# The last four row chunks of an FFN output: from plain products to a seven-product group of eight

## The chip, the cores and the metric

The kernel runs on one core of a Trainium2 chip. The core has five engines that work side by side and meet at semaphores: TensorE (PE, matmuls; PEld is its loading of weights), VectorE (DVE), ScalarE (ACT), GpSimd (POOL) and SyncE (SP). Transfers are issued from the queues of SP, ACT and POOL. The metric is device time in microseconds, the median of several runs.

## The reference

One layer of a streaming encoder over 1024 tokens with 1024 channels, all in f32: a modulation from `c`, a mixing sub-layer of two causal convolution branches, and a feed-forward (FFN) sub-layer, each added to `x`; at the end an RMS norm. The part that matters here:

```python
x = x + g1 * mix
h2 = rms_norm(x, norm_ffn_g[l]) * (1.0 + sc2) + sh2
a, bgate = jnp.split(jnp.einsum('bsd,df->bsf', h2, w_ffn_in[l]), 2, axis=-1)
x = x + g2 * jnp.einsum('bsf,fd->bsd', jax.nn.silu(a) * bgate, w_ffn_out[l])
...
return rms_norm(x, final_norm_g)
```

The hidden width is 2816, which is 22 row chunks of 128. The output of the FFN is a product of (22 chunks x 1024 tokens) with (22 chunks x 1024 output channels).

## The kernel before, in words

**Operands.** Channels lie on the 128 partitions and tokens along the row; the 1024 tokens are two halves of 512. Each f32 operand is split into a high and a low part that TensorE takes as fp32r, so one block of a product is three matmuls: high by high, low by high, high by low (`mm3`, lines 394, 395 and 397). Weights are loaded into raw buffers by SP, cast to the high part by ACT (line 231), and the low part is formed by DVE (line 232).

**Seven products.** Most matrix products go by a scheme of Strassen's kind: a 2 x 2 block product from seven block products instead of eight. A "dual" is such a block product for two sets of output rows; its products are named 1 to 7 and run in the order `PRODUCTS = "1265734"`. Operand and weight sums are made beforehand (for weights by `dual_units`: three sums before product 6, one before product 3). Products 1, 6, 7, 4 add up in the banks "x", 5 and 3 in the banks "z", 2 goes to "y"; after each product DVE reads the bank and adds it, scaled, into the residual. As 7 adds into the banks that 6 left, and 3 into those of 5, PE can't begin a product before the earlier one of its banks has been read.

**The in stage.** Eleven duals (`in_product`, d = 0 to 10) make the 22 hidden chunks, a pair of them each. After each dual, `hid_set(d)` stores the pair to DRAM scratch: for d up to 8 it forms four sums and makes seven stores, the seven operands that the out stage's products want. The last two pairs (`2 * d >= REST`) are stored plainly, four stores each. A store is a cast (ACT, line 434), a subtraction (DVE, line 435) into one of three "stage" buffers, and a DMA from POOL's queue (line 1314). While the last dual runs, `group_load(0, m)` begins to load operands for the out stage, also from POOL's queue (line 1340).

**The residual.** Right after the in stage, POOL's queue loads x after the mixing sub-layer, eight tiles `x1` (two at line 1398, earlier; six at line 1403 in the order 4, 5, 2, 3, 6, 7). Those six lie in a pool that is opened when the pools "gi" (work tiles of the in stage) and "stage" are closed; the pools are opened so that each tile waits for the very tiles that it lies on.

**The out stage.** Three groups (`GROUPS`) of `GROUP = 3` pairs, that is 18 row chunks; per group two duals (d = 0 for outputs 0, 1, 4, 5; d = 1 for 2, 3, 6, 7) with 7 products of 18 matmuls of 512 tokens (line 397 and its fellows). DVE's `out_evac` (line 1410) adds each bank to x1. The operands of a group (`to`) lie in the pool "t" of 58 tiles of 512 columns; those of the next group are loaded as buffers come free.

**The pieces.** The last four chunks (`REST` to `FC`) are multiplied plainly, from weights `ws` split ahead of time, in three pieces of tokens, `PIECES`: 512, 256 and 256. For each piece and each of eight outputs `piece_out` runs 4 x 3 matmuls, adds the result to x1 (line 1461), squares it (ACT, line 1464) and sums the squares (DVE, line 1473). The final norm and the scaled output of one piece run beside the matmuls of the next (`piece_norm`, `piece_rstd`, `piece_scale`); those of the last piece come after the last matmul, with POOL scaling outputs `POOL_LAST` and DVE the others.

**What sets the order.** The program gives each engine's instructions in the order of the program text where they are ready, and passes over those that are not; `tc.issue_after` forces an order in places. Weights come from a list `plan`; `next_w` keeps two units prepared ahead of the product that runs. In the end every engine and every DMA queue runs its own list in order, so whatever waits at the head of a queue holds all behind it.

Of the kernel before, what the change touches and what calls it, by code (L numbers as in the profile page):

```python
# [120 lines left out]
PIECES = [(0, 512), (512, 256), (768, 256)]  # L123


FILL = 248
# [1 line left out]

@with_exitstack
def block_kernel(ctx: ExitStack, tc: tile.TileContext, x0, xT, c, vecs, ada, w_first, w_plain, w_duals,  # L130
                 w_short, w_conf, w_o, w_fi, w_fo, w_last, outT):
    nc = tc.nc

    def pool(name, bufs, **kw):
# [14 lines left out]
    rawp = pool("raw", 3)  # L149
# [51 lines left out]
    def modc(i):  # L201
        return mod[:, i : i + 1]
# [1 line left out]

    raws = [rawp] * 3 + [rawbp] * 2

    def raw_tile(n=1024):

        raws.append(raws.pop(0))
        return raws[-1].tile([P, 1024], F32, tag="raw", name="raw")[:, :n]  # L210

    def load(src, n=1024):
        raw = raw_tile(n)
# [126 lines left out]
    plan = [None] * KC  # L340
# [14 lines left out]
    def next_w(ahead=AHEAD):  # L355

        fetch(ahead + 1)
        return ready.pop(0)
# [27 lines left out]
    def mm3(outs, wsl, w, xs, first, last, again=False):  # L386

        if w[1] is None:
            for ps, x in zip(outs, xs):
                mm3.ins = nc.tensor.matmul(ps, w[0][:, wsl], x, start=first, stop=last, skip_group_check=again).ins  # L390
            return
        wh, wl = w[0][:, wsl], w[1][:, wsl]
        for ps, (xh, xl) in zip(outs, xs):
            nc.tensor.matmul(ps, wh, xh, start=first, stop=False, skip_group_check=again)  # L394
            nc.tensor.matmul(ps, wh, xl, start=False, stop=False, skip_group_check=again)  # L395
        for ps, (xh, _) in zip(outs, xs):
            mm3.ins = nc.tensor.matmul(ps, wl, xh, start=False, stop=last, skip_group_check=again).ins  # L397
# [32 lines left out]
    def t_pair(name):  # L430
        return hl_tile(name + "h"), hl_tile(name + "l")

    def t_split(src, hi, lo):
        t_split.act = nc.scalar.copy(hi, src).ins  # L434
        t_split.ins = nc.vector.tensor_tensor(lo, src, f32(hi), ALU.subtract).ins  # L435
# [873 lines left out]
    def store(key, src):  # L1309

        s = stagep.tile([P, T], F32R, tag="stage", name="stage")
        t_split(src, s[:, :H], s[:, H:])
        hid_dram[key] = dram.tile([P, T], F32R, name="hid" + "_".join(map(str, key)))
        nc.gpsimd.dma_start(hid_dram[key], s)  # L1314

    def hid_set(d):

        (b11, b12), (b21, b22) = ((ha[2 * d + p, "4"], ha[2 * d + p, "6"]) for p in range(2))
        if 2 * d >= REST:
            for p, half in enumerate(((b11, b12), (b21, b22))):  # L1320
                for h in range(2):
                    store((2 * d + p, h), half[h])
            return
        store((d, "1"), b11)
        store((d, "2"), b21)
        t2 = gip.tile([P, H], F32, tag="g", name="t2")
        nc.vector.tensor_tensor(b11, b11, b12, ALU.subtract)
        minus(t2, b11, b22)
        store((d, "6"), t2)
        store((d, "5"), b11)  # L1330
        nc.vector.tensor_tensor(b12, b22, b12, ALU.subtract)
        store((d, "7"), b12)
        store((d, "3"), b22)
        minus(b21, t2, b21)
        store((d, "4"), b21)

    def t_load(key):
        hl = t_pair("t")
        for t, s in zip(hl, halves):
            nc.gpsimd.dma_start(t, hid_dram[key][:, s])  # L1340
        return hl
# [1 line left out]
    to = {}  # L1343

    def group_load(g, m):
        to[g, m] = [t_load((g * GROUP + i, m)) for i in range(GROUP)]

    def in_product(d, m, between=None):
        late = EARLY[d] == 1
# [20 lines left out]
    for i, (d, m) in enumerate(in_order[5:]):  # L1370
        if i < 4:
            norm_2_sums("5734"[i])
        elif i == 4:
            close(*phase_1)
            raws.append(open_pool("raw_a", 1, side="right", stack=ctx)[1])
            x1aps = [s2p, open_pool("x1a", 1, side="right", stack=ctx)[1]]
            phase_2 = [open_pool("gi", 7), open_pool("stage", 3, side="right")]
            gip, stagep = (p for _, p in phase_2)
        with ExitStack() as order:
            if d < 2:  # L1380
                order.enter_context(tc.issue_after(mm3.ins))
            in_product(d, m)
        if m == PRODUCTS[-1]:
            if 2 <= d < 6:
                with tc.issue_after(in_evac.ins):
                    for b in range(40 + 2 * (d - 2), 42 + 2 * (d - 2)):
                        modulation(b, x1aps[b % 2].tile([P, T], F32, tag="x1", name="ada"))
            if d:
                hid_set(d)
        elif (d, m) == (1, "6"):  # L1390
            hid_set(0)
# [20 lines left out]
            )  # L1412
        return evac

    hid = {}
    n = 2 * GROUP * P
    for g in range(GROUPS):
        for d in range(2):
            units = dual_units([w_fo[g, d, m] for m in range(4)], n)
            plan += [units[m] for m in PRODUCTS]  # L1420
    for g in range(GROUPS):
        for d in range(2):
            banks = {}
            for m in PRODUCTS:
                product(banks, m, to[g, m], out_evac(d))
                if d == 0 and m == "1":
                    if g < GROUPS - 1:
                        for q in PRODUCTS:
                            group_load(g + 1, q)
                    else:  # L1430
                        for h in range(2):
                            for f in range(REST, FC):
                                hid[f, h] = t_load((f, h))


    ws = {}
    for f in range(REST, FC, 2):
        for oh in range(2):
            raw = load(w_last[(f - REST) // 2, oh])
            for d in range(2):  # L1440
                ws[f + d, oh] = t_pair("lw")
                t_split(raw[:, d * H : (d + 1) * H], *ws[f + d, oh])

    LAST = len(PIECES) - 1

# [3 lines left out]
    def on_pool(i, j):  # L1449
        return i < LAST or j in POOL_LAST  # L1450

    def piece_out(i, j):
        at, n = PIECES[i]
        h, off = at // H, at % H
        o = ps_tile("y")[:, :n]
        for f in range(REST, FC):
            xs = tuple(t[:, off : off + n] for t in hid[f, h])
            c0 = (j % 4) * P
            mm3([o], slice(c0, c0 + P), ws[f, j // 4], [xs], f == REST, f == FC - 1)
        dst = x1[j][:, at : at + n]  # L1460
        evac = nc.vector.scalar_tensor_tensor(out=dst, in0=o, scalar=modc(40 + j), in1=dst, op0=ALU.mult, op1=ALU.add)
        piece_out.ins = evac.ins
        sq = wide_tile("sq")[:, :n]
        act = nc.scalar.activation(sq, dst, AF.Square, scale=1.0 / 32.0)
        if i == LAST and j == KC - 1:
# [3 lines left out]
        sqs.append(sq)  # L1469

    def piece_sum(i, j):
        with tc.issue_after(piece_out.ins):
            nc.vector.tensor_tensor(sqs[0], sqs[0], sqs[j], ALU.add)

    def piece_scale(i, rf):
# [39 lines left out]
    for i in range(len(PIECES)):  # L1515
        acc, sqs = sqs[0] if i else None, []
        lag = LAG if i == LAST else 0
        for j in range(KC):
            piece_out(i, j)
            if j > lag and j - lag < KC - APART * (i == LAST):  # L1520
                piece_sum(i, j - lag)
            if i and j == NORM_AT:
                norm = piece_norm(i - 1, [acc])
            if i and j == NORM_AT + 2:
                with tc.issue_after(piece_out.ins):
                    rf = piece_rstd(i - 1, *norm)
                piece_scale(i - 1, rf)
    piece_scale(LAST, piece_rstd(LAST, *piece_norm(LAST, [sqs[0]] + sqs[KC - APART :])))


# [69 lines left out]
```

## Time and profile before

| | us |
|---|---|
| median of 3 runs (lowest, highest) | 1468.06 (1467.23, 1470.21) |
| the profiled execution: its time | 1467.47 |
| the profiled execution: its span | 1465.7 |
| PE busy | 1452.6 |
| DVE busy | 1181.2 |
| ACT busy | 624.5 |
| POOL busy | 505.7 |

The span runs from the first to the last instruction; the profiled execution's time is 1.8 us longer. The profile is a page with busy times, the chain of work that ended last, and groups of instructions by line; behind it one can ask for the instructions of an engine in order of time (start, duration, engine, line, operation, and in brackets the idle time before it and what ended that), for one tile or line, and for busy times by stretch. In a row of stretches the columns are the stretch, its length, and the busy time of PE, PEld, DVE, ACT and POOL, each with its count, then the granted clock, the busy share of the DMA engines and GB/s. Matmuls overlap, so their spacing, not their duration, is the price of one.

### The profile page before, as it was taken

The numbers are of one execution on the slowest core, as the hardware profiler recorded it, in microseconds if no ns is written. First come the engines' busy times: TensorE is split into PE (matmuls) and PEld (weight loads), VectorE is DVE, ScalarE is ACT, GpSimd is POOL, SyncE is SP. The second block draws the span as 40 slices with busy tenths as digits, with TensorE's granted clock in tenths as the row PEclk, the third lists the DMA queues.
The fourth block names the chain that finished last, engine by engine and source line by source line (L and its number), as shares of the span: only waits on it lengthen the run. The fifth ranks groups of instructions, "written<-read, shape, count | busy, mean of one in ns | idle before, by whom it ended". The sixth has DMA issues, their size and how long they took to land.

```text
span 1465.7 us, 17762 instructions
## 1 busy us (share of the span) xinstructions
PE 1452.6 (99%) x6418; PEld 1192.7 (81%) x6418; DVE 1181.2 (81%) x1642; ACT 624.5 (43%) x911; POOL 505.7 (35%) x460
## 2 busy tenths in 40 slices
PE   9999999999999999999999999999999999999997
PEld 5788888888888888888888888888888888888887
DVE  8897999987988979999787798777777665676755
ACT  4873333333333346455225474434444343222335
POOL 0007777677767761111012002101111015435005
PEclk9999999999999999999999999999999999999999
DMA  9442222323222367485585337655554449989403
GB/s 369 172 156 82 73 101 72 115 72 101 72 101 58 130 204 269 130 267 191 198 326 191 118 116 238 221 181 193 169 170 149 146 155 373 353 276 288 137 11 115
DMA packets 85498, 251.38 MB, mean 172 GB/s; under 512 B 9841, under 2 KB 12529, under 8 KB 85410
## 3 DMA queue, kind: packets, MB, share of 16 engines
q1 hardware_dynamic: 44368, 142.04, 29.2%
q0 software_dynamic: 37008, 95.63, 19.7%
q10 hardware_dynamic: 4034, 12.59, 2.3%
q8 instruction: 50, 0.82, 0.2%
q14 instruction: 38, 0.31, 0.1%
HBM read 187.82 MB, written 62.39 MB: 171 GB/s over the span
## 4 chain that ended last, share of the span: by engine, by line
PE 88%; DVE 1%; POOL 1%; issue 1%; DMA 0%; ACT 0%; POOLq 0%; DVEq 0%
PE bank L397 11%; PE bank L394 11%; PE bank L395 11%; PE x L395 8%; PE x L397 8%; PE x L394 8%; PE z L395 4%; PE z L394 4%; PE z L397 4%; PE y L394 3%; PE y L395 3%; PE y L397 3%; PE mix L394 2%; PE mix L395 2%; PE yb L395 2%; PE yb L397 2%
## 5 line engine op out<-in xcount | busy, mean ns | idle before, releaser
L231 ACT CAST wh<-raw 128x1024 fp32r<-128x1024 f32 (+3 forms) x256 | 256.4, 1003 | 469.7 <-PE bank L395 145.9
L232 DVE TENSOR_TENSOR wl<-raw,wh 128x1024 fp32r<-128x1024 f32 (+3 forms) x176 | 201.1, 1143 | 54.0 <-ACT wh L231 52.7
L232 POOL TENSOR_TENSOR wl<-raw,wh 128x1024 fp32r<-128x1024 f32 x80 | 194.0, 2427 | 103.9 <-ACT wh L231 100.7
L964 DVE SCALAR_TENSOR_TENSOR c<-diff,vec,c 128x512 f32<-128x512 f32 x232 | 168.3, 751 | 2.7
L1314 POOL DMA_DIRECT2D hid<-stage x71 | 37.8, 533 | 344.7 <-DVE stage L435 340.7
L397 PE MATMUL bank<-th,wl 128*128 128x512 f32 x312 | 121.6, 390 | 0.3 <-POOL wl L232 0.3
L395 PE MATMUL bank<-tl,wh 128*128 128x512 f32 x312 | 121.5, 390 | 0.0
L394 PE MATMUL bank<-th,wh 128*128 128x512 f32 x312 | 121.5, 389 | 0.0
L964 DVE SCALAR_TENSOR_TENSOR c<-u,wsum,c 128x512 f32<-128x512 f32 x112 | 84.3, 753 | 2.3
L397 PEld LDWEIGHTS bank<-th,wl 128*128 128x128 f32 x312 | 58.6, 188 | 12.8 <-POOL wl L232 0.7
L395 PEld LDWEIGHTS bank<-tl,wh 128*128 128x128 f32 x312 | 58.6, 188 | 12.2
L394 PEld LDWEIGHTS bank<-th,wh 128*128 128x128 f32 x312 | 58.6, 188 | 12.0
L434 ACT CAST stage<-g 128x512 fp32r<-128x512 f32 x62 | 38.3, 621 | 63.5 <-DMA hid<-stage 40.2
L435 DVE TENSOR_TENSOR stage<-g,stage 128x512 fp32r<-128x512 f32 x62 | 42.4, 689 | 26.9 <-ACT stage L434 26.8
L309 POOL TENSOR_TENSOR raw<-raw 128x1024 f32<-128x1024 f32 x8 | 20.5, 2561 | 109.7 <-ACT th L434 104.7
L397 PE MATMUL x<-th,wl 128*128 128x512 f32 x144 | 56.1, 390 | 0.0
L395 PE MATMUL x<-tl,wh 128*128 128x512 f32 x144 | 56.1, 389 | 0.0
L394 PE MATMUL x<-th,wh 128*128 128x512 f32 x144 | 56.1, 389 | 0.0
L1340 POOL DMA_DIRECT2D th<-hid x71 | 38.1, 536 | 51.4 <-PE x L397 33.1
L397 PE MATMUL yb<-zsh,wl 128*128 128x512 f32 x128 | 49.9, 390 | 0.0
L394 PE MATMUL yb<-zsh,wh 128*128 128x512 f32 x128 | 49.9, 389 | 0.0
L395 PE MATMUL yb<-zsl,wh 128*128 128x512 f32 x128 | 49.8, 389 | 0.0
(817 smaller groups left out, 4175.1 us busy)
## 6 DMA issues: line engine op xcount, KB each, us to landing
hid<-stage POOLq DMA_DIRECT2D x71, 512.0 KB, 4.8
raw<-in_w_duals SPq DMA_DIRECT2D x57, 512.0 KB, 3.5
raw<-in_w_fi SPq DMA_DIRECT2D x54, 512.0 KB, 4.5
th<-hid POOLq DMA_DIRECT2D x71, 256.0 KB, 5.6
tl<-hid POOLq DMA_DIRECT2D x71, 256.0 KB, 5.7
ada<-in_ada SPq DMA_DIRECT2D x24, 512.0 KB, 5.7
raw<-in_ada SPq DMA_DIRECT2D x24, 512.0 KB, 4.8
raw<-in_w_fo SPq DMA_DIRECT2D x24, 384.0 KB, 5.8
```

The source lines that it names most:

```text
L231: hi = nc.scalar.copy(wh, raw)
L232: lo = lo_engine.tensor_tensor(wl, raw, f32(wh), ALU.subtract)
L309: unit.eng.tensor_tensor(out, x, y, ALU.add)
L394: nc.tensor.matmul(ps, wh, xh, start=first, stop=False, skip_group_check=again)
L395: nc.tensor.matmul(ps, wh, xl, start=False, stop=False, skip_group_check=again)
L397: mm3.ins = nc.tensor.matmul(ps, wl, xh, start=False, stop=last, skip_group_check=again).ins
L434: t_split.act = nc.scalar.copy(hi, src).ins
L435: t_split.ins = nc.vector.tensor_tensor(lo, src, f32(hi), ALU.subtract).ins
L964: tap.ins = nc.vector.scalar_tensor_tensor(out=out, in0=src[:, s : s + H], scalar=wt, in1=acc, op0=ALU.mult, op1=ALU.add).ins
L1314: nc.gpsimd.dma_start(hid_dram[key], s)
L1340: nc.gpsimd.dma_start(t, hid_dram[key][:, s])
```

## The change

All 22 chunks of the FFN's output go by seven products, in groups of 3, 4 and 4 pairs (`GROUPS = 3, 4, 4`). The plain rest with its weights `w_last` is gone, and so are the plain stores: all eleven pairs make four sums and seven stores each.

The first two groups run as before, the second with 24 matmuls per product and weights of 1024 columns. The last group runs in another order: products 1, 2, 6, 7, 4 of dual 0, then the same of dual 1 (512 tokens each), and then products 5 and 3 of both duals in the two pieces of 256 tokens: 5 of dual 0, 5 of dual 1, 3 of dual 0, 3 of dual 1. After 2 and 4 the outputs of the first half of the tokens are complete, after 5 and 3 those of a piece, in the order 4, 5, 6, 7, 0, 1, 2, 3; `piece_done` then does what `piece_out` did behind its matmuls. `POOL_LAST` becomes 1, 4, 7.

The weights of products 5 of dual 1 and 3 of both duals stay in the three weight buffers over both pieces. Those of 5 of dual 0 are split into four tiles of the pool "t" instead (`split_5`), ahead of the sums for product 6 of dual 1, whose first sum takes the raw buffer that held them.

```diff
-POOL_LAST = (0, 3, 5)
+POOL_LAST = (1, 4, 7)
-GROUP, GROUPS = 3, 3
-REST = 2 * GROUP * GROUPS
+GROUPS = 3, 4, 4
+FIRST = [sum(GROUPS[:g]) for g in range(len(GROUPS))]
+LAST_PRODUCTS = "12674"
...
     def hid_set(d):
-        if 2 * d >= REST:
-            for p, half in enumerate(((b11, b12), (b21, b22))):
-                for h in range(2):
-                    store((2 * d + p, h), half[h])
-            return
         store((d, "1"), b11)
...
+    def last_units(mats, first):
+        a, homes = {}, dict(zip(("11", "12", "21", "22"), (rawp, rawbp, rawp, rawp) if first else (rawap, rawp, rawp, rawp)))
...
+            if m == "6":
+                if not first:
+                    split_5()
+                a["s1"] = raw_tile(home=rawbp)
+                add(a["s1"], a["21"], a["22"])
+                add(a["21"], a["21"], a["11"])
+                add(a["11"], a["11"], a["s1"])
+            w = split_w(a[{"1": "11", "2": "12", "6": "11", "7": "21", "4": "22", "5": "s1", "3": "12"}[m]], 1024)
+            if m == "6":
+                add(a["12"], a["12"], a["11"])
+            return w
...
+    def split_5():
+        for p in range(2):
+            w5.append(t_pair("w5"))
+            t_split(last[0]["a"]["s1"][:, p * H : (p + 1) * H], *w5[p])
...
+    plan += [last[d][m] for d in range(2) for m in LAST_PRODUCTS]
+    plan += [last[d][m] for m, d in (("5", 1), ("3", 0), ("3", 1))]
...
+    def piece_product(banks, d, m, i):
+        at, n = PIECES[i]
+        off = at % H
+        apart = (d, m) == (0, "5")
+        for p in range(2):
+            if m == "5":
+                banks[d, p] = ps_tile("z")[:, :n]
+            ps = banks[d, p]
+            for k in range(KH):
+                xs = tuple(t[:, off : off + n] for t in to[FINAL, m][k])
+                c0 = ((0 if apart else p) * KH + k) * P
+                mm3([ps], slice(c0, c0 + P), w5[p] if apart else ws[d, m], [xs], m == "5" and k == 0, k == KH - 1, m == "3")
+            last_evac(d, i)(p, m, ps)
...
+    for d in range(2):
+        banks = {}
+        for m in LAST_PRODUCTS:
+            product(banks, m, to[FINAL, m], last_evac(d, 0))
+    ws = {}
+    for i in range(1, len(PIECES)):
+        banks = {}
+        for m in "53":
+            for d in range(2):
+                if i == 1 and (d, m) != (0, "5"):
+                    ws[d, m] = next_w()
+                piece_product(banks, d, m, i)
```

More of the change, by code (lines that the diff above doesn't have):

```diff
@@ L205, in block_kernel, with raw_tile, load @@
     raws = [rawp] * 3 + [rawbp] * 2
[L207 to L213, printed above, removed]
+    def raw_tile(n=1024, home=None):
+        if home is None:
+            raws.append(raws.pop(0))
+        return (home or raws[-1]).tile([P, 1024], F32, tag="raw", name="raw")[:, :n]
+    def load(src, n=1024, home=None):
+        raw = raw_tile(n, home)
         with tc.issue_after(x1_load[0]) if x1_load else ExitStack():
@@ L1345, in group_load @@
     def group_load(g, m):
-        to[g, m] = [t_load((g * GROUP + i, m)) for i in range(GROUP)]
+        to[g, m] = [t_load((FIRST[g] + i, m)) for i in range(GROUPS[g])]
     def in_product(d, m, between=None):
@@ L1413, in out_evac, with add, unit @@
         return evac
-    hid = {}
-    n = 2 * GROUP * P
-    for g in range(GROUPS):
+    def last_units(mats, first):
+        a, homes = {}, dict(zip(("11", "12", "21", "22"), (rawp, rawbp, rawp, rawp) if first else (rawap, rawp, rawp, rawp)))
+        def add(out, x, y):
+            nc.vector.tensor_tensor(out, x, y, ALU.add)
+        def unit(m):
+            if m == "1":
+                for i, (b, home) in enumerate(homes.items()):
+                    a[b] = load(mats[i], home=home)
+            if m == "6":
[9 more added lines that the diff above has]
+            return w
+        return {m: (lambda m=m: unit(m)) for m in PRODUCTS} | {"a": a}
+    def split_5():
+        for p in range(2):
+            w5.append(t_pair("w5"))
+            t_split(last[0]["a"]["s1"][:, p * H : (p + 1) * H], *w5[p])
+    w5 = []
+    FINAL = len(GROUPS) - 1
+    for g in range(FINAL):
+        n = 2 * GROUPS[g] * P
         for d in range(2):
-            units = dual_units([w_fo[g, d, m] for m in range(4)], n)
+            units = dual_units([(w_fo0[d, m] if g == 0 else w_fo1[g - 1, d, m]) for m in range(4)], n)
             plan += [units[m] for m in PRODUCTS]
-    for g in range(GROUPS):
+    last = [last_units([w_fo1[FINAL - 1, d, m] for m in range(4)], d == 0) for d in range(2)]
+    plan += [last[d][m] for d in range(2) for m in LAST_PRODUCTS]
+    plan += [last[d][m] for m, d in (("5", 1), ("3", 0), ("3", 1))]
+    for g in range(FINAL):
         for d in range(2):
@@ L1426, in block_kernel @@
                 if d == 0 and m == "1":
[L1427 to L1442, printed above, removed]
+                    for q in PRODUCTS:
+                        group_load(g + 1, q)
     LAST = len(PIECES) - 1
@@ L1450, in on_pool, with piece_done @@
         return i < LAST or j in POOL_LAST
-    def piece_out(i, j):
+    def piece_done(i, j):
+        nonlocal norm, acc
         at, n = PIECES[i]
[L1454 to L1459, printed above, removed]
         dst = x1[j][:, at : at + n]
-        evac = nc.vector.scalar_tensor_tensor(out=dst, in0=o, scalar=modc(40 + j), in1=dst, op0=ALU.mult, op1=ALU.add)
-        piece_out.ins = evac.ins
         sq = wide_tile("sq")[:, :n]
         act = nc.scalar.activation(sq, dst, AF.Square, scale=1.0 / 32.0)
-        if i == LAST and j == KC - 1:
+        sqs.append(sq)
+        c = len(sqs) - 1
+        if i == LAST and c == KC - 1:
             load_rsqrt(act.ins)
@@ L1513, in piece_rstd @@
         return out
[L1515 to L1527, printed above, removed]
+    norm, acc, sqs = None, None, []
+    for d in range(2):
[10 more added lines that the diff above has]
+                piece_product(banks, d, m, i)
     piece_scale(LAST, piece_rstd(LAST, *piece_norm(LAST, [sqs[0]] + sqs[KC - APART :])))
@@ L1571, with out_duals @@
     w_fi, w_fo = i["w_ffn_in"][0], i["w_ffn_out"][0]
+    def out_duals(g):
+        ks = [range(2 * FIRST[g] + n, 2 * (FIRST[g] + GROUPS[g]), 2) for n in range(2)]
+        return _duals(w_fo, [range(4), range(4, 8)], ks)
     arrays = {
```

37 lines of the change are left out of this document (30 added, 7 removed).

## The prediction

> **What bounds the kernel now.** I read the page's busy shares and the chain that ended last first, then the stretch of the FFN's output (1237 to 1456 us), then, engine by engine, the places the diff touches.
>
> ```profile
> span 1465.7 us, 17762 instructions
> PE 1452.6 (99%) x6418; PEld 1192.7 (81%) x6418; DVE 1181.2 (81%) x1642; ACT 624.5 (43%) x911; POOL 505.7 (35%) x460
> ...
> PE 88%; DVE 1%; POOL 1%; issue 1%; DMA 0%; ACT 0%; POOLq 0%; DVEq 0%
> ```
>
> 88% of the chain is matmul. The table of stretches shows the same for this one: PE busy in all 219.00 us, the other engines with room.
>
> ```profile
> 1237.00:1456.00 219.00, 219.00 (x1056) 184.97 (x1055) 148.85 (x203) 65.83 (x101) 72.85 (x124) 1.00 0.63 204
> ```
>
> So a matmul taken away is worth its spacing, as long as nothing that PE waits for comes later. The order of time on PE gives the spacing: first matmul of one product of group 2 and first of the next (18 apart), then the first and the last of 24 matmuls of 256 tokens.
>
> ```profile
> 1384.48 0.39 PE L394 MATMUL y<-th,wh 128*128 128x512 f32 x1
> ...
> 1388.56 0.39 PE L394 MATMUL x<-th,wh 128*128 128x512 f32 x1
> ...
> 1430.72 0.28 PE L394 MATMUL y<-th,lwh 128*128 128x256 f32 x1
> ...
> 1433.47 0.28 PE L397 MATMUL y<-th,lwl 128*128 128x256 f32 x1
> ```
>
> 4.08 / 18 = 0.227 us for 512 tokens, 2.75 / 23 = 0.120 us for 256.
>
> **The change, part by part.**
>
> *Fewer matmuls.* Before: 3 groups x 2 duals x 7 products x 18 matmuls = 756, and the plain rest 8 outputs x 4 chunks x 3 = 96 of 512 tokens and 192 of 256. After: 252 + 336 + 240 = 828 of 512 tokens (the last group has five whole products per dual), and 2 pieces x 4 products x 24 = 192 of 256. The 192 stay; 852 become 828. Gain: 24 x 0.227 = 5.4 us, all on the path.
>
> *Hidden chunks of the last two pairs.* Each pair now makes seven stores with four sums, where it made four stores. Three more stores cost ACT 3 x 0.62 and DVE 3 x 0.69 us, four sums DVE about 4 x 0.69 us: time that DVE has. But the stores go through a ring of three stage buffers, each free again only when its DMA has landed. POOL's order of time shows a pair with seven stores (1162 to 1177) and the last pair with four, with the loads of the residual x (L1403) behind it:
>
> ```profile
> 1162.33 0.53 POOL L1314 DMA_DIRECT2D hid<-stage  x1 [24.41 <-DVE stage L435]
> 1166.60 1.73 POOL L1314 DMA_DIRECT2D hid<-stage  x3 [3.74 <-DVE stage L435]
> 1171.89 0.53 POOL L1314 DMA_DIRECT2D hid<-stage  x1 [3.55 <-DVE stage L435]
> 1174.42 0.53 POOL L1314 DMA_DIRECT2D hid<-stage  x1 [2.00 <-DVE stage L435]
> 1176.75 0.53 POOL L1314 DMA_DIRECT2D hid<-stage  x1 [1.80 <-DVE stage L435]
> ...
> 1238.07 1.13 POOL L1314 DMA_DIRECT2D hid<-stage  x2 [1.06 <-DVE stage L435]
> 1241.71 0.53 POOL L1314 DMA_DIRECT2D hid<-stage  x1 [2.52 <-DVE stage L435]
> ...
> 1244.41 0.54 POOL L1314 DMA_DIRECT2D hid<-stage  x1 [1.10 <-DVE stage L435]
> 1244.93 0.55 POOL L1340 DMA_DIRECT2D th<-hid  x1
> 1245.45 0.56 POOL L1340 DMA_DIRECT2D tl<-hid  x1
> 1245.97 0.57 POOL L1340 DMA_DIRECT2D th<-hid  x1
> 1246.49 0.58 POOL L1403 DMA_DIRECT2D x<-x_dram  x1
> 1252.49 2.61 POOL L1403 DMA_DIRECT2D x<-x_dram  x5 [5.42 <-issue]
> ```
>
> Five of the six loads of x leave at 1252.49, after a wait that the profile gives no releaser for. The view of the stage tile, for the store of 1244.41 alone, has its landing (first row); the view of line 1403 has the wait, on a semaphore (second row):
>
> ```profile
> DMA to landing us min/median/max: 7.6/7.6/7.6
> ```
>
> ```profile
> L1403 POOLq EVENT_SEMAPHORE  x3: 17/17/5678, 1245.8 to 1252.5; - x3
> ```
>
> 1244.41 + 0.5 + 7.6 = 1252.5: I read this as the load of x[5] waiting for the last store, whose buffer lies where the x tiles are opened (the pools gi and stage are closed for them). The order of the loads, 4, 5, 2, 3, 6, 7, is not touched. Who waits for x: DVE's evacuations of product 5 (out<-z), and behind them PE, which adds product 3 into the same banks.
>
> ```profile
> 1256.65 0.75 DVE L1410 SCALAR_TENSOR_TENSOR x<-z,ng,x 128x512 f32<-128x512 f32 x1 [4.99 <-DMA x<-x_dram]
> 1258.59 0.75 DVE L1410 SCALAR_TENSOR_TENSOR x<-z,ng,x 128x512 f32<-128x512 f32 x1 [1.18 <-DMA x<-x_dram]
> ...
> 1261.12 0.74 DVE L1410 SCALAR_TENSOR_TENSOR x<-x,ng,x 128x512 f32<-128x512 f32 x1
> ```
>
> ```profile
> 1260.01 0.39 PE L394 MATMUL z<-th,wh 128*128 128x512 f32 x1
> ...
> 1262.06 0.39 PE L394 MATMUL x<-th,wh 128*128 128x512 f32 x1
> ```
>
> DVE already stood 4.99 us for x[4] and 1.18 us for x[5]. The second evacuation ends at 1259.34 and PE needs it at 1260.01: 0.67 us of cover. The evacuation of product 7, queued behind, ends at 1261.86 and PE needs it at 1262.06: 0.20 us. That is all that hides these loads, so a later last store stalls PE by nearly all its delay.
>
> How much later? In the pair of seven, first to last store is 1176.75 - 1162.33 = 14.42 us, in the last pair 1244.41 - 1238.07 = 6.34: 8.1 us more. In the seven, the last one waits for one landing (the fourth store's). Landings of the seven, then of the four:
>
> ```profile
> DMA to landing us min/median/max: 2.9/4.2/6.1
> ```
>
> ```profile
> DMA to landing us min/median/max: 4.1/5.6/7.6
> ```
>
> Around the last pair the DMA engines are nearly full (its view from 1236 to 1262 us):
>
> ```profile
> DMA packets 3549, 9.59 MB, mean 369 GB/s; under 512 B 392, under 2 KB 392, under 8 KB 3548
> ```
>
> so I price the one turn of the ring like that window: 5.6 - 4.2 = 1.4 us more. With the last store's own landing and that of x[5] as now, x[5] comes 8.1 + 1.4 = 9.5 us later, and PE stalls 9.5 - 0.2 = 9.3 us. Bounds: below, no stall (if x is not behind the last store); above, 18 us (third rival).
>
> [...]
>
> *The pair before the last* also has three stores more, beside the last pair's matmuls, as the pair of seven shown above had its stores beside the next pair's; 0, covered like those.
>
> *Groups of 8.* Costs by line, out of the stretch from 1180 us on:
>
> ```profile
> L1410 DVE SCALAR_TENSOR_TENSOR x<-x,mod,x 128x512 f32<-128x512 f32 x24 | 17.9, 750 | 14.3 <-PE x L397 14.3
> ...
> L232 DVE TENSOR_TENSOR wl<-raw,wh 128x1024 fp32r<-128x1024 f32 x9 | 11.0, 1225 | 14.0 <-ACT wh L231 13.7
> ...
> L231 ACT CAST wh<-raw 128x1024 fp32r<-128x1024 f32 x8 | 8.4, 1049 | 15.0 <-PE z L395 7.6 <-PE y L395 3.9 <-PE x L395 3.4
> ...
> L435 DVE TENSOR_TENSOR lwl<-raw,lwh 128x512 fp32r<-128x512 f32 x8 | 5.5, 689 | 1.4 <-ACT lwh L434 1.0 <-PE x L395 0.4
> ...
> L434 ACT CAST lwh<-raw 128x512 fp32r<-128x512 f32 x8 | 4.8, 621 | 5.0 <-DMA raw<-in_w_last 2.4 <-PE x L395 1.8 <-PE y L395 0.7
> ...
> L251 DVE TENSOR_TENSOR raw<-raw 128x1024 f32<-128x1024 f32 x1 | 1.2, 1224 | 0.0
> ```
>
> A product takes PE 24 x 0.227 = 5.44 us and DVE 2 x 0.75 + 1.23 + 4/7 x 1.22 = 3.4 us: hidden. Activations: 28 pairs of 512 KB a group, 4 freed per product, 2.1 MB in 5.44 us = 385 GB/s. That is a little over the 369 GB/s shown, but each is needed only seven products after its buffer is free; 0. POOL issues 12 loads more, some 0.5 us each, with 146 of the 219 us free; 0. The queue of SP has as many bytes of weights as before.
>
> *Last group, second dual, product 6.* Its weights wait for a chain. Product 5's weights of the first dual must first go from the raw buffer into four "t" tiles, and with 56 of 58 taken these come free half-way through the second half of the second dual's product 1. From then: cast 0.62, subtraction 0.69, three sums 3.67, cast 1.05, subtraction 1.23 = 7.3 us. PE needs the result after 6 x 0.227 + 24 x 0.227 + 2 x 0.227 = 7.3 us. One evacuation (0.75) between them makes it late: I take 0.7 us, from 0 to 2.3 (three evacuations).
>
> *Pieces and end.* As many matmuls and evacuations per piece as now; order of outputs 4 to 7, 0 to 3, but POOL's share keeps the places 0, 3, 5 of that order. Eight small weight splits go. 0, give or take 0.5 us at the tail.
>
> **Sum**, against the profiled execution (1467.47 us, span 1465.7 and 1.8 around it; 0.6 under the median of the three runs): -5.4 + 9.3 + 0.7 = +4.6 us, so 1468.06 + 4.6 = 1472.7 us for the median.
>
> **The rivals.**
>
> *First, short landings (no measurable change).* If turn and last store land in the seven's median, 4.2 us, the stall is 9.3 - 1.4 - (7.6 - 4.2) = 4.5 us; -5.4 + 4.5 + 0.7 = -0.2: 1467.9 us. For it: POOL's queue may be emptier while it waits for stores. Against: 369 GB/s in that window. Going on to landings near the shortest shown, 2.9 us, takes 2 x 1.3 us more and, with a quick x[5], nearly all the rest: 1463.4 us. [...]
>
> *Second, x not behind the last store (faster).* If the tiles of x[4] and x[5] lie over buffers that earlier stores free, evacuations keep their times and only -5.4 + 0.7 is left: 1463.4 us. It decides as soon as x[5] comes less than 2 us later than now. For it: x[4] left at 1246.49, not waiting for the landing. Against: x[5] did wait, and pools and order are the same.
>
> *Third, POOL's queue fills ahead of x (slower still).* Three loads of group 1 (1244.93 to 1245.97) went before x[4] already; with the last store 9 us later up to 13 more can, 13 x 0.26 MB at 369 GB/s = 9 us. Half of that: a stall of 14 us, 1477 us; all of it 18 us. Against: such loads would be moved while POOL waits anyway.
>
> **How the numbers follow.** Bound for a change that shows: 0.2%, 2.9 us. Forecast 0.43 (own range 1470.0 to 1475.5; 0.35 of it over 1471.0, 0.08 under); short landings 0.24, the shortest 0.05; second 0.18; third 0.10. Slower 0.35 + 0.10 = 0.45, same 0.08 + 0.24 = 0.32, faster 0.23. The range, 1462.8 to 1477.0, takes in both sides and leaves out the worse half of the third and some of the second.
>
> **What would show it.** Right: seven stores in the last pair, the last at about 1254 us; x[5] leaving about 9 us later; a gap on PE just before product 3 or 4 of group 0's first dual; later, a gap under 1 us before product 6 of the last group's second dual; 6394 matmuls; from the last matmul to the end as now. Wrong: no gap on PE near 1260 us, or one under 5.4 us.

## The result, and the profile after

The changed kernel takes 1471.81 us (median) against 1468.16 us: ratio 1.0023, 95% interval 1.0013 to 1.0032, so 3.65 us slower. Forecast were 1472.7 us and +4.6.

The page of the changed kernel, with the chain that ended last:

```profile
span 1471.6 us, 17717 instructions
...
PE 1452.9 (99%) x6394; PEld 1190.1 (81%) x6394; DVE 1189.2 (81%) x1633; ACT 628.3 (43%) x910; POOL 515.8 (35%) x478
...
PE 85%; DVE 2%; POOL 1%; DMA 1%; issue 1%; ACT 0%; POOLq 0%; DVEq 0%; ACTq 0%
```

6394 matmuls: the 24 are gone. PE's share of the chain fell from 88% to 85%. The profiled execution (1473.45 us) began its first product 2.8 us later than that of the kernel before (at 18.88 instead of 16.09 us), where no line differs. At product 3 of the last dual of the in stage it is 3.1 us behind (1229.78 instead of 1226.69). Below, "late start" is this second difference: 0.9 us in run one, 1.6 in two, 2.0 in three, 0.4 in five, 1.2 in seven and in nine, 1.7 in ten.

POOL's order of time around the last pair (start, duration, operation, and in brackets the wait before it):

```profile
1245.22 1.81 POOL L1316 DMA_DIRECT2D hid<-stage  x3
...
1254.46 0.53 POOL L1316 DMA_DIRECT2D hid<-stage  x1 [6.80 <-DVE stage L437]
...
1261.20 0.53 POOL L1316 DMA_DIRECT2D hid<-stage  x1 [0.89 <-PE x L397]
...
1263.29 0.57 POOL L1401 DMA_DIRECT2D x<-x_dram  x1
1266.27 2.08 POOL L1401 DMA_DIRECT2D x<-x_dram  x4 [2.40 <-issue]
```

The last store leaves at 1261.20 instead of 1244.41, x[5] at 1266.27 instead of 1252.49: 13.8 us later, 10.7 of them without the late start. What hangs on them stands in the orders of time of ACT, DVE and PE:

```profile
1252.82 0.62 ACT L436 CAST stage<-g 128x512 fp32r<-128x512 f32 x1 [3.13 <-DMA hid<-stage]
...
1259.56 0.62 ACT L436 CAST stage<-g 128x512 fp32r<-128x512 f32 x1 [1.32 <-DMA hid<-stage]
1260.09 1.78 ACT L233 CAST wh<-raw 128x768 fp32r<-128x768 f32 x2
```

```profile
1262.46 0.96 DVE L253 TENSOR_TENSOR raw<-raw 128x768 f32<-128x768 f32 x1 [0.55 <-DMA raw<-in_w_fo]
...
1264.33 0.95 DVE L234 TENSOR_TENSOR wl<-raw,wh 128x768 fp32r<-128x768 f32 x1
...
1270.66 0.75 DVE L1408 SCALAR_TENSOR_TENSOR x<-z,ng,x 128x512 f32<-128x512 f32 x1 [4.38 <-DMA x<-x_dram]
```

```profile
1260.83 0.39 PE L399 MATMUL x<-th,wl 128*128 128x512 f32 x1
1261.92 0.50 PE L396 MATMUL x<-th,wh 128*128 128x512 f32 x1 [0.70 <-ACT wh L233]
...
1262.73 0.40 PE L397 MATMUL x<-tl,wh 128*128 128x512 f32 x1
1265.34 0.79 PE L399 MATMUL x<-th,wl 128*128 128x512 f32 x1 [2.21 <-DVE wl L234]
1265.93 0.63 PE L396 MATMUL x<-th,wh 128*128 128x512 f32 x1
...
1271.05 0.54 PE L399 MATMUL x<-th,wl 128*128 128x512 f32 x1
...
1272.51 0.40 PE L396 MATMUL z<-th,wh 128*128 128x512 f32 x1
```

In this program the scheduler put product 1 of the second dual ahead of product 3 of the first. So PE first waits for its weights: the four casts of stores stand in ACT's queue ahead of them, each waiting for a landing (3.13, 1.53, 1.29 and 1.32 us), and `wl` stands in DVE's queue behind the sum at 1262.46, which waits for a load of weights. After the gap PE runs at half clock (0.50, last section) to 1271.05, and x[4]'s evacuation ends at 1271.41, just ahead of `z` at 1272.51. From 1260.83 to 1272.51 there are 20 matmuls in 11.68 us; at 0.227 us each they would take 4.54: 7.1 us lost. Below, "PE lost" is this excess of the spacings over 0.227 us, summed over 1200 to 1300 us of PE's order of time: 7.2 us here, 0.0 in the kernel before.

At the end (PE, then DVE):

```profile
1451.12 0.28 PE L399 MATMUL z<-th,w5l 128*128 128x256 f32 x1
1452.31 0.70 PE L1554 MATMUL ss<-sq,ones 128*128 128x256 f32 x2 [0.91 <-DVE sq L1526]
...
1461.36 0.28 PE L399 MATMUL z<-th,wl 128*128 128x256 f32 x1
```

```profile
1447.53 3.31 DVE L1526 TENSOR_TENSOR sq<-sq 128x256 f32<-128x256 f32 x3
```

A wait of 0.91 us that the kernel before does not have: DVE's sums of squares come late in piece 2. From the last matmul to the end of the span are 10.2 us (10.6 before).

The sum by the profiled executions: late start +3.1, PE lost in group 0 +7.2, product 6 of the last group +0.3 (two matmuls, one of 256 tokens and one of 512, take 0.66 us from 1420.48 on where 0.35 would do), the wait in piece 2 +0.9, the tail -0.4, 24 matmuls -5.4: +5.7 (the spans differ by 5.9). Without the late start +2.6, against +3.65 of the medians, whose interval goes from 1.9 to 4.7.

### The profile page after: what moved, and what is told of

The parts are those of the page before. It is cut to its first block, busy times and chain, and to the rows that moved or that the text cites. A ratio compares the mean times of both kernels' runs of the same rounds, so it can differ in the third digit from the quotient of the medians.

```text
span 1471.6 us, 17717 instructions
## 1 busy us (share of the span) xinstructions
PE 1452.9 (99%) x6394; PEld 1190.1 (81%) x6394; DVE 1189.2 (81%) x1633; ACT 628.3 (43%) x910; POOL 515.8 (35%) x478
## 4 chain that ended last, share of the span: by engine, by line
PE 85%; DVE 2%; POOL 1%; DMA 1%; issue 1%; ACT 0%; POOLq 0%; DVEq 0%; ACTq 0%
PE bank L399 11%; PE bank L397 11%; PE bank L396 11%; PE x L399 8%; PE x L397 8%; PE x L396 8%; PE z L396 4%; PE z L397 4%; PE z L399 4%; PE y L396 2%; PE y L397 2%; PE y L399 2%; PE mix L396 2%; PE mix L399 2%; PE yb L396 2%; PE yb L397 2%
## 5 line engine op out<-in xcount | busy, mean ns | idle before, releaser
L233 ACT CAST wh<-raw 128x1024 fp32r<-128x1024 f32 (+3 forms) x255 | 261.3, 1026 | 472.8 <-PE bank L397 147.3
L234 DVE TENSOR_TENSOR wl<-raw,wh 128x1024 fp32r<-128x1024 f32 (+3 forms) x175 | 209.4, 1197 | 49.8 <-ACT wh L233 47.1
L1316 POOL DMA_DIRECT2D hid<-stage x77 | 41.0, 533 | 354.5 <-DVE stage L437 350.1
L437 DVE TENSOR_TENSOR stage<-g,stage 128x512 fp32r<-128x512 f32 x66 | 45.4, 690 | 33.6 <-ACT stage L436 33.5
L399 PE MATMUL x<-th,wl 128*128 128x512 f32 x176 | 69.8, 399 | 2.2 <-DVE wl L234 2.2
L396 PE MATMUL x<-th,wh 128*128 128x512 f32 x176 | 69.6, 396 | 0.7 <-ACT wh L233 0.7
L397 PE MATMUL x<-tl,wh 128*128 128x512 f32 x176 | 69.5, 395 | 0.0
L1337 POOL DMA_DIRECT2D th<-hid x77 | 41.1, 534 | 57.7 <-PE x L399 34.0
```

What stands on the lines that cost most here:

```text
L233: hi = nc.scalar.copy(wh, raw)
L234: lo = lo_engine.tensor_tensor(wl, raw, f32(wh), ALU.subtract)
```

## The experiments

The first four were to show that the last pair's ring makes the stall.

**One: the stores of the last pair alone, in the kernel before.**

```
+        if d == N_IN - 1:
+            ...            # four sums, seven stores, three of them read by nobody
+            return
         if 2 * d >= REST:
```

> The kernel before with its own products and groups; only the last pair of hidden chunks is changed: it makes the four sums and seven stores through the ring of three stage buffers (three of the stores are read by nobody; the output stays the reference's). My theory, that the seven stores of the last pair make the stall in group 0: 7 to 9 us over the kernel before, 1475 to 1477 us, with the last store of the pair near 1260 us, x[5] leaving 10 us or more later than before and PE standing 7 us in group 0. The rival, that the loss of the changed kernel sits in its groups of 8, its split for product 5 or its pieces: 1468 us, within 1 us of the kernel before.

Measured: 1478.38 us against 1468.54, ratio 1.0064 (1.0052 to 1.0076): 9.8 us; PE lost 10.3. The orders of time of POOL, DVE and PE:

```profile
1255.37 0.53 POOL L1314 DMA_DIRECT2D hid_x<-stage  x1 [0.94 <-DVE stage L435]
...
1260.41 2.61 POOL L1417 DMA_DIRECT2D x<-x_dram  x5 [2.38 <-DMA hid_x<-stage]
```

```profile
1264.78 0.96 DVE L251 TENSOR_TENSOR raw<-raw 128x768 f32<-128x768 f32 x1 [6.65 <-DMA raw<-in_w_fo]
```

```profile
1259.81 0.39 PE L397 MATMUL x<-th,wl 128*128 128x512 f32 x1
1267.49 0.77 PE L394 MATMUL z<-th,wh 128*128 128x512 f32 x1 [7.29 <-issue]
```

The prediction priced exactly this edit at 9.3 us, and the gap is where it put it, before product 3. x[5] waits for the last store's landing (the releaser stands in the row). One thing is new: DVE waits 6.65 us for a load of weights, ahead of x's evacuations. Without that wait x would have held PE nearly as long: x[4], which left at 1257.46, landed 8.3 us later, at 1265.8, and the two sums of weights ended at 1266.65.

**Two: the changed kernel with four stores in the last pair.**

```
+        if d == N_IN - 1:
+            for m, b in zip("1265", (b11, b21, b12, b22)):
+                store((d, m), b)
+            for m in "734":
+                hid_dram[d, m] = hid_dram[d, "5"]
+            return
```

> The changed kernel with only four stores and no sums in the last pair; products 7, 3 and 4 read the tile stored for product 5 of that pair, so that part of the output is left out. Everything else, the products and their loads too, is as in the changed kernel. My theory: the stall of 7.2 us in group 0 is gone, x[5] leaves near 1252 us, and what is left is the gain of 5.4 us less 0.5 (product 6 of the last group) and 0.9 (the wait before the sum of squares in piece 2): 1464 us (1463 to 1465.5). The rival: stays within 1.5 us of the changed kernel, 1470 to 1473 us.

Measured: 1472.24 us, ratio 1.0022 (1.0013 to 1.0031); PE lost 8.6. My theory fell: what alone costs 9.8 us gives nothing back when it alone is undone. POOL:

```profile
1247.41 0.54 POOL L1316 DMA_DIRECT2D hid<-stage  x1 [0.96 <-DMA th<-hid]
...
1255.62 0.53 POOL L1316 DMA_DIRECT2D hid<-stage  x1 [5.68 <-DVE stage L437]
```

The first store of the last pair leaves at 1247.41 instead of 1238.07 (1.6 of it the late start): group 0's loads, ahead of it in POOL's queue, were late already.

**Three: the seven stores past the ring.**

```
+        hid_dram[key] = dram.tile([P, T], F32R, name="hid" + "_".join(map(str, key)))
+        if key[0] == N_IN - 1 and key[1] in "5734":
+            hl = t_pair("t") if key[1] == "4" else [gsp.tile([P, H], F32R, tag="gs", name="gst") for _ in range(2)]
+            t_split(src, *hl)
+            for t, s in zip(hl, halves):
+                nc.gpsimd.dma_start(hid_dram[key][:, s], t)
+            return
...
-        hid_dram[key] = dram.tile([P, T], F32R, name="hid" + "_".join(map(str, key)))
```

> The changed kernel with all seven stores and four sums of the last pair, but stores four to seven not through the ring: three go out of pairs of the gs tiles (free by then) and one out of a pair of t tiles, each as two transfers of 256 KB. No store waits for a landing any more. My theory, that the ring's waits for landings make the stall (through the casts queued on ACT behind them and through the loads of x behind the last store): 1464 us (1463 to 1466), faster than both kernels. The rival, that the bytes themselves do it (seven stores of 512 KB beside the loads of group 0 keep the DMA engines full, and x lands late whatever the tiles): 1469 to 1472 us.

Measured: 1471.18 us, ratio 1.0020 (1.0011 to 1.0028); PE lost 7.7. The time is the rival's. POOL, then DVE, then a table of stretches (busy us of PE, PEld, DVE, ACT, POOL, then granted clock, DMA share, GB/s):

```profile
1254.69 1.05 POOL L1407 DMA_DIRECT2D x<-x_dram  x2 [0.70 <-DMA raw<-in_w_fo]
```

```profile
1263.13 0.96 DVE L253 TENSOR_TENSOR raw<-raw 128x768 f32<-128x768 f32 x1 [4.97 <-DMA raw<-in_w_fo]
```

```profile
1240.00:1250.00 10.00, 9.91 (x44) 7.86 (x44) 9.97 (x16) 5.99 (x10) 7.66 (x15) 1.00 1.21 406
1250.00:1260.00 10.00, 10.00 (x46) 8.28 (x45) 5.15 (x7) 1.67 (x2) 4.25 (x9) 1.00 1.15 395
1260.00:1270.00 10.00, 5.75 (x16) 3.95 (x15) 6.29 (x8) 0.83 (x1) 3.72 (x7) 0.73 1.07 413
```

x[5] now leaves 11.6 us earlier than in the changed kernel (1.1 of them the difference of the late starts), and next to nothing comes of it: the sum ahead of the weights of product 1 waits for the fourth load of weights. That load left at 1254.33 and landed 8.7 us later, 384 KB, while the engines moved 395 to 413 GB/s; the last such load of the kernel before landed in 6.2 us. And x[4], at 1253.45, still leaves 4.9 us later than in the kernel before, late start apart, and lands after 10.3 us, at 1263.8. DVE was busy for 9.97 of the 10 us in which most of the seven subtractions and four sums came at once; run eight shows what that is worth.

**Four: the same, with x held back on POOL.**

```
+    pad = gip.tile([P, H], F32, tag="g", name="pad")
+    nc.gpsimd.memset(pad, 1.0)
+    for _ in range(10):
+        nc.gpsimd.tensor_tensor(pad, pad, pad, ALU.mult)
     close(*phase_2)
```

> The kernel with the stores out of other tiles, and ten multiplications of 128x512 on POOL (nobody reads their result) ahead of the six loads of x in POOL's queue: about 10 x 1.35 = 13.5 us by the scaling of x in the profile. So the loads of x leave about as late as in the changed kernel, near 1266 us, but no cast on ACT waits for a landing. If late x is what stops PE: a stall before product 3 of group 0's first dual or thereabouts, 4 to 8 us over the kernel with other tiles, 1468 to 1472 us. If the casts of weights queued on ACT behind casts of stores are what stops PE, and late x alone is covered since product 1 and 2 of the second dual can go ahead: within 2 us of the kernel with other tiles, 1464 to 1466 us.

Measured: 1478.27 us, ratio 1.0075 (1.0056 to 1.0094); 7.1 us over run three, and over both of the expected times, which were counted from 1464. Six loads of x left at 1269.44 instead of 1253.45. But the run doesn't show that late x stops PE. x[4] landed after 4.3 us, at 1273.7, and its evacuation begins at 1278.19, behind a split of weights in DVE's queue. PE's longest wait, 5.81 us, is for another split, behind sums that took 1.68 us and more beside POOL's multiplications (last section). That late x alone can stop PE is shown by run nine.

The next four took up the full DMA engines.

**Five: four stores in both of the last pairs** (the diff of run two, with `d >= N_IN - 2`).

> The changed kernel with four stores and no sums in both of the last two pairs, as the kernel before has them; products 7, 3 and 4 read the tile stored for product 5 of those pairs, so that part of the output is left out. New theory (the runs before showed the stall of 7 to 9 us staying when the last pair alone goes back to four stores, or past the ring): from the pair before the last on, POOL's queue and the DMA engines are full until group 0 runs (350 to 400 GB/s from 1210 to 1260 us), so every store added in either of the two pairs, 0.52 MB at 369 GB/s = 1.4 us each, makes what comes behind it late: 6 x 1.4 = 8.5 us. Then here the stall is gone: 1464 us (1463 to 1465.5). The rival, that the groups of 8 and their loads make the stall: 1470 to 1473 us.

Measured: 1463.55 us against 1468.65, ratio 0.9967 (0.9954 to 0.9979); PE lost 0.0. POOL and DVE:

```profile
1251.46 2.61 POOL L1407 DMA_DIRECT2D x<-x_dram  x5 [1.68 <-DMA hid<-stage]
```

```profile
1256.08 0.75 DVE L1414 SCALAR_TENSOR_TENSOR x<-z,ng,x 128x512 f32<-128x512 f32 x1 [4.05 <-DMA x<-x_dram]
```

As in the kernel before, to within a microsecond. The groups of 8 and their loads cost nothing here; the stall comes from the stores of the two pairs.

**Six: the bytes alone, badly placed.**

```
+            for i in range(3):
+                nc.gpsimd.dma_start(dram.tile([P, T], F32, name=f"extra{d}{i}"), cs)
```

> The kernel before with three more transfers of 512 KB from a constant tile to scratch memory behind the stores of each of the last two pairs, six in all; no stage buffer, no cast, no sum and no reader hangs on them. Only POOL's queue and the bytes grow, as much as by the six more stores of the change. If the bytes are what makes the stall: 6 x 0.52 MB at 369 GB/s = 8.5 us, less the little that is covered: 7 to 9 us over the kernel before, 1475 to 1477 us. If the ring's waits for landings, or the casts and sums on ACT and DVE, are needed for it: under 2.5 us, 1468 to 1470.5 us.

Measured: 1474.00 us, ratio 1.0034 (1.0022 to 1.0047). That looked like the theory, and is not its proof; POOL's order of time shows where the six went:

```profile
10.56 3.17 POOL L1324 DMA_DIRECT2D extra<-cs  x6 [7.63 <-DVE sq L547]
```

Their source was ready at the start, so the scheduler issued them there, beside the first loads. PE lost 0.6 us in 1200 to 1300 and some 6 us more than before in the first 100 us. Of the stall this run says nothing.

**Seven: seven stores in the pair before the last alone, in the kernel before** (the diff of run one, with `d == N_IN - 2`).

> The kernel before with seven stores and four sums in the pair before the last alone (three of the stores read by nobody, the output stays the reference's); the last pair makes four as before. The prediction put this pair's three more stores at 0, covered. If that was right: within 1 us of the kernel before, 1468 us. If they delay the loads of group 0 in POOL's queue, and behind those the stores of the last pair and the loads of x: 3 x 0.52 MB at 369 GB/s = 4.3 us at least, and more where the ring of the last pair adds a wait: 1472 to 1477 us.

Measured: 1475.22 us, ratio 1.0037 (1.0023 to 1.0051): 6.6 us; PE lost 7.2. The prediction's 0 for this pair was wrong. POOL:

```profile
1243.98 1.79 POOL L1314 DMA_DIRECT2D hid<-stage  x3
...
1253.82 0.53 POOL L1314 DMA_DIRECT2D hid<-stage  x1 [6.26 <-DVE stage L435]
```

The last pair has its four stores as before, but the first leaves 5.9 us later and the last 9.4 (1.2 of each is the late start).

**Eight: fewer bytes.** Group 0 takes pairs 0, 1 and the last; the last pair's blocks go straight into `t` tiles.

```
-FIRST = [sum(GROUPS[:g]) for g in range(len(GROUPS))]
+CHUNKS = [[0, 1, 10], [2, 3, 4, 5], [6, 7, 8, 9]]
...
+        if key[0] == N_IN - 1:
+            to[0, key[1]].append(t_pair("t"))
+            t_split(src, *to[0, key[1]][-1])
+            return
...
-        to[g, m] = [t_load((FIRST[g] + i, m)) for i in range(GROUPS[g])]
+        to[g, m] = [t_load((c, m)) for c in CHUNKS[g] if c < N_IN - 1]
...
-        ks = [range(2 * FIRST[g] + n, 2 * (FIRST[g] + GROUPS[g]), 2) for n in range(2)]
+        ks = [[2 * c + n for c in CHUNKS[g]] for n in range(2)]
```

> The changed kernel with the groups filled in another order: group 0 takes pairs 0, 1 and the last pair, groups 1 and 2 take pairs 2 to 9. The last pair's seven split blocks are written straight into t tiles and never stored or loaded: 7 stores and 14 loads (3.67 MB each) are gone from the stretch in which the DMA engines are full, and x waits for no store of the last pair. By the theory of full DMA engines the stall is gone, with 3 x 0.52 MB of the pair before the last more than covered by the 7.3 MB less: 1464 us (1462.5 to 1466), faster than both kernels. The rival: product 1 or 2 of group 0 waits for the last pair's casts on ACT and DVE at the border of the two stages, 2 to 4 us, 1466 to 1468 us.

Measured: 1463.15 us, ratio 0.9963 (0.9950 to 0.9975), PE lost 0.0: faster than both kernels, with all seven products. POOL, and the stretch that was full in run three:

```profile
1244.58 2.10 POOL L1405 DMA_DIRECT2D x<-x_dram  x4 [11.06 <-DVE tl L437]
```

```profile
1240.00:1250.00 10.00, 10.00 (x46) 8.28 (x45) 10.00 (x16) 4.90 (x9) 3.53 (x7) 1.00 0.50 170
```

x leaves at 1244.58 and the engines move 170 GB/s instead of 406. DVE is as full as in run three, and PE does not wait: DVE's work alone is not the stall. Nor did PE wait at the border of the stages.

**Nine and ten: the bytes alone, in their place.** Twelve transfers of 256 KB from `g` tiles of the pair before the last, on POOL's queue (nine) and on SP's (ten).

```
+            if d == N_IN - 2:
+                for i in range(12):
+                    nc.gpsimd.dma_start(dram.tile([P, H], F32, name=f"extra{i}"), (b11, b21)[i % 2])   # ten: nc.sync
```

> The kernel before with twelve more transfers of 256 KB (3.1 MB, as many bytes as the change's six more stores) beside the stores of the pair before the last, from that pair's own g tiles to scratch memory, on POOL's queue. In the run before this one the six transfers had a constant tile as source and left at 10.6 us, in the first stage; a source that is only made at 1200 us keeps them in their place. No stage buffer, cast or sum hangs on them. If bytes and POOL's queue ahead of the loads of group 0 make the stall: 6 to 9 us over the kernel before, 1474 to 1477 us. If the ring, the casts or the sums are needed: under 2 us, 1468 to 1470 us.

> The same twelve transfers from the same tiles on SP's queue, where no activation, store or x waits behind them: the DMA engines carry the same bytes, POOL's queue is as in the kernel before. If full DMA engines make the stall: as with POOL's queue, 1474 to 1477 us. If it is the place in POOL's queue (each issue there waits for the landing of an older one): within 1.5 us of the kernel before, 1468 to 1470 us.

Measured: 1473.58 us (1.0027, 1.0016 to 1.0038) and 1474.12 us (1.0033, 1.0022 to 1.0045): 4.8 and 5.3 us; PE lost 5.9 and 5.3. ACT and PE of ten:

```profile
1250.47 0.62 ACT L434 CAST stage<-g 128x512 fp32r<-128x512 f32 x1 [6.29 <-DMA hid<-stage]
```

```profile
1259.40 0.39 PE L397 MATMUL x<-th,wl 128*128 128x512 f32 x1
1263.32 0.76 PE L394 MATMUL z<-th,wh 128*128 128x512 f32 x1 [3.52 <-issue]
```

In ten POOL has not one instruction more, no store, cast or sum is added, and the stall stands in the same place. So added bytes alone are enough for a stall of 5 to 6 us; the queue they leave from makes no difference that these intervals can tell. Nor does each issue on POOL's queue wait for a landing, as the expectation of ten has it: of the 142 loads of line 1340 in the kernel before, 11 stood idle until one. 3.1 MB at 369 GB/s are 8.5 us; 5 to 6 arrive on PE. The expected 6 us and more was a little high.

The path is the prediction's. With the same four stores, the cast for the last one waits 6.29 us for a landing in the ring (in the kernel before it follows at 1242.42 without such a wait), the store leaves at 1252.11 instead of 1244.41 (1.7 of it the late start), x[4] behind it at 1254.21 instead of 1246.49, and x[4] lands at 1262.4. In nine the releasers show that x then stops PE (DVE, then PE):

```profile
1265.19 0.75 DVE L1413 SCALAR_TENSOR_TENSOR x<-z,ng,x 128x512 f32<-128x512 f32 x1 [2.80 <-DMA x<-x_dram]
```

```profile
1265.99 0.50 PE L394 MATMUL z<-th,wh 128*128 128x512 f32 x1 [2.43 <-DVE x L1413]
```

**Eleven: four stores in the pair before the last, seven in the last** (the diff of run two, with `d == N_IN - 2`).

> The changed kernel with four stores and no sums in the pair before the last alone, seven in the last pair; products 7, 3 and 4 read the tile stored for product 5 of the pair before the last, so that part of the output is left out. With the runs so far this fills the table of both pairs in the changed kernel: seven and seven 1471.8, seven and four 1472.2, four and four 1463.6 us. As the prediction priced it (the last pair alone makes the stall): 1471 to 1474 us. If the pair before the last alone makes it: 1463 to 1466 us.

Measured: 1474.01 us, ratio 1.0032 (1.0022 to 1.0043); PE lost 10.4. The changed kernel by stores of the two pairs: seven and seven 1471.8, seven and four 1472.2, four and seven 1474.0, four and four 1463.6. Either pair alone makes a stall as long as both together. That seven and seven is not the worst may come from the order on PE, where there product 1 of the second dual (18 x 0.227 = 4.1 us) runs ahead of `z`, and in eleven one matmul of it; this is read from the two orders and not shown.

**Twelve: the wait in piece 2**, on top of eight.

```
-        if i and c == NORM_AT:
+        if i and c == NORM_AT + (i == LAST):
```

> The kernel that keeps the last pair's blocks in t tiles, with the sum of squares of piece 1 (the matmuls of ss) put behind the third instead of the second output of piece 2. The wait of 0.91 us for DVE's sums before it should be gone: 1462.3 us, 0.9 us under the kernel that keeps the blocks (1463.2). If POOL's scaling then ends later than the last piece's square root, the tail takes it back: 1463 us.

Measured: 1462.79 us against 1468.83, ratio 0.9956 (0.9941 to 0.9970), the fastest. PE now goes from the last matmul ahead of `ss` to `ss` without a wait, and the tail is the 10.3 us of run eight. Between eight and twelve the medians differ by 0.4 us, less than the intervals can tell.

## Why the prediction was right, and where it was not

**Fewer matmuls, -5.4 us:** right. In run five, where the stall is gone, 1.1 us of small gaps (piece 2 and product 6), a late start of 0.4 and a tail shorter by 0.3 leave -4.2 of it; the span fell from 1465.7 to 1461.5 us, 4.2.

**The last pair's stores, +9.3 us:** alone, in run one, 9.8 by the medians and 10.3 on PE. In the changed kernel 7.2. The mechanism was half of the truth: the last store and x did come later as priced (10.7 us for x[5], where 9.5 stood), but the term was read as this pair's alone. Nor are the bytes the whole of it where one pair has seven stores: three more are 1.57 MB, 4.3 us at 369 GB/s, and runs one and seven lost 10.3 and 7.2 us. In run one two casts wait 2.28 and 4.04 us for landings in the ring, in run seven one waits 4.44; how much of the stall is the ring's was not measured apart.

**The pair before the last, "0, covered like those":** this is the step that failed. Alone it costs 6.6 us (run seven). The cover it named, the next pair's matmuls, hid these stores' casts and sums (run eight has them, and PE lost 0.0), but not the bytes (5.3 us in run ten): behind these stores come 42 loads of group 0, and the engines are full from there until group 0 runs. They were as full in the kernel before, so what is added there makes the rest late. The tables of stretches of the changed kernel and, second, of the kernel before:

```profile
1210.00:1220.00 10.00, 10.00 (x45) 8.29 (x45) 4.88 (x8) 4.43 (x7) 3.89 (x9) 1.00 1.11 350
...
1250.00:1260.00 10.00, 10.00 (x46) 8.29 (x45) 5.03 (x7) 3.04 (x5) 1.81 (x4) 1.00 1.10 393
```

```profile
1180.00:1190.00 10.00, 10.00 (x46) 8.29 (x45) 5.18 (x7) 4.13 (x6) 0.00 (x0) 1.00 0.21 59
...
1210.00:1220.00 10.00, 10.00 (x46) 8.29 (x45) 4.43 (x5) 3.76 (x5) 5.02 (x10) 1.00 1.18 382
```

The earlier pair of seven that it was compared with (1162 to 1177 us) had no loads of group 0 behind it: 59 GB/s follow. So the total came near by luck in this term: two causes, each enough by itself, stood in one place. Added they would have made 9.3 + 6.6; together they made 7.2, and the prediction had counted one.

**"Time that DVE has":** true of the mean, not of the place; run three shows DVE full from 1240 to 1250 us (9.97 of 10 us) and the splits of weights behind it.

**Where the stall shows:** the prediction named product 3 or 4 of the first dual, with the last store at about 1254 us; that store left at 1261.20 (3.1 of it the late start), and in the changed kernel the gap came before product 1 of the second, through weights, with x just behind. In the kernels that keep the old order on PE (one, seven, ten) it stands before product 3.

**Product 6 of the last group, +0.7:** about 0.3; PE filled the gap in part with matmuls of product 5. **Pieces and end, 0 give or take 0.5 at the tail:** the tail was right, and a wait of 0.9 us in piece 2 was missed.

**The rivals.** Short landings: in the view of the stage tile, the last pair's seven stores landed in 4.3 to 11.0 us, median 5.0, and not in the 4.2 us, or at the shortest 2.9, that the rival takes. Second: x[5] did wait for the last store, as run one's releaser shows (the prediction's 1244.41 + 0.5 + 7.6 counts the issue twice, as landings count from its start). Third: only three loads went between the last store and x[4], as before.

## What to carry to other kernels

Where a change adds transfers, look at the GB/s of the stretch they fall into and of what queues behind it, not at the engine that issues them: in a stretch at 350 to 400 GB/s 3.1 MB more cost 4.8 to 5.3 us, paid by what arrived last. When several arrivals are late together, undoing one of them can return nothing (1472.2 and 1474.0 us in runs two and eleven, against 1471.8), so a null result of such a run does not clear it; add each one alone to the kernel before as well. And look in the trace where an added probe really ran (run six) before its time is believed.

## What the runs showed of the hardware

After the gap in group 0 PE ran at half rate. The changed kernel's table of stretches, 2 us each:

```profile
1262.00:1264.00 2.00, 1.13 (x4) 0.59 (x4) 1.50 (x2) 0.00 (x0) 1.86 (x4) 1.00 1.07 317
...
1266.00:1268.00 2.00, 2.00 (x6) 1.58 (x5) 0.28 (x1) 0.00 (x0) 1.74 (x4) 0.50 1.12 342
1268.00:1270.00 2.00, 2.00 (x6) 1.55 (x5) 0.00 (x0) 0.00 (x0) 1.50 (x4) 0.50 1.02 391
```

The granted clock is 0.50 and the matmuls stand 0.43 us apart (1265.93 to 1271.05) after a wait of 2.21 us; some 12 matmuls x 0.2 = 2.4 us of the 7.2 are this. Ahead of that wait stood one of 0.70 us, after which the clock was still 1.00 (1262 to 1264); how long a wait has to be for the clock to fall was not measured.

DVE was slower beside POOL's arithmetic. In run four, during POOL's multiplications (POOL busy 1.98 of the 2 us from 1262):

```profile
1262.91 1.68 DVE L256 TENSOR_TENSOR raw<-raw 128x768 f32<-128x768 f32 x1
```

A sum of this kind and shape takes 0.96 us in run three (1263.13, above). The three sums of 256 tokens at 1447.53 above (3.31 us, 1.1 each), beside POOL's scaling, are of the same kind: the same sum takes 0.42 us at 1440.68, where POOL is idle.
